# Dilated values: stored order in group 0, 512 columns wide in groups 1 and 2, made between the last latent blocks; four gates between dilated blocks

## The chip, the cores and the metric

One core of one Trainium2 chip runs the whole program. The metric is the device time of one execution in microseconds (us); several executions are summed up by their median. TensorE (PE) multiplies, ScalarE (ACT) and VectorE (DVE) do the arithmetic around it, GpSimd (POOL) casts and fills a few tiles, and SyncE (SP) issues nearly all loads from memory.

## The reference, cut to what matters

Four layers work on 512 tokens of 1024 features. Only the first two, of one kind (`first_block`), are touched by the change. In each of them a normalised input `h` is multiplied by `w_in`, and three kinds of attention read the product; each result is projected, multiplied by a gate and added up:

```python
y_a = mla_mixer(c_q, c_kv, k_r, ...)              # latent attention, 8 heads
y_b = dilated_mixer(q_b, k_b, qkv_b[:, :, 2])     # 12 heads: 3 groups of 4, dilation 1, 4, 16
y_c = neighbourhood_mixer(qkv_c[:, :, 0], ...)    # 8 heads
gates = sigmoid(gate_logits).reshape(B, S, 3, D_MODEL)
merged = gates[:, :, 0] * (y_a @ w_pa[l]) + gates[:, :, 1] * (y_b @ w_pb[l]) + gates[:, :, 2] * (y_c @ w_pc[l])
x = x + merged @ w_o[l]
```

The values of the dilated attention are `h @ w_in` at 3 x 256 columns (group 0, 1, 2). A query of group 0 sees keys within 64 tokens; in group 1 tokens whose numbers agree modulo 4 see each other, in group 2 modulo 16. A softmax over the three groups' log sums weights their outputs, which is the same as one softmax over all the keys of the three groups together, and so the kernel does it.

## The kernel before, in words

The tokens are stored in an order `NA_TOK` that suits the neighbourhood attention. `h` lies in SBUF transposed: eight tiles of 128 features x 512 tokens, each split into a high and a low part (`r` tiles, fp32r), and each product is three matmuls (`mm3`: high by high, high by low, low by high). Weights are streamed: SP loads 128 x 1024 numbers into one of three `raw` tiles, ACT casts the high part into one of two `whi` tiles, DVE subtracts the low part into `wlo`, and 24 matmuls read them (a unit).

A layer runs three pipelines of attention blocks one after the other: `mla` (latent, 32 blocks), `dil` (dilated, 4 head positions `j` x 4 query blocks `b` = 16 blocks) and `na` (neighbourhood, 32 blocks). Each block has a `before` list (work that is written ahead of it), a `score` part and a `rest` part, which follows one or two blocks later. The order on each engine is not the order in which the code is written: a scheduler sorts the instructions when the program is built, and can pull matmuls that wait for nothing in among earlier attention blocks.

`vproj` makes values: `h` is the stationary operand (128 features x 128 tokens are loaded into PE), 256 columns of weights stream past it. For the three dilated groups (`order4`) a token block is every fourth stored token (`m4(a)[:, b]`), so the 128 numbers of a partition that PE loads lie four elements (16 bytes) apart. For the neighbourhood's two groups the 128 tokens lie side by side. A group is 8 feature tiles x 4 token blocks x 3 matmuls = 96 matmuls. All three dilated groups are written ahead of the first dilated block. `roped` makes the rotated queries and keys, and writes them in the same order by four.

A gate is one unit (`gate`): 24 matmuls of 512 columns, a DVE multiplication by the norm, an ACT tanh. The gates of the dilated branch are made in `merge(1, ...)`, which runs as a filler inside the neighbourhood blocks.

PSUM has eight banks, in two lists: `AB` (five) for attention blocks, `MB` (three) for everything else. Lists of tiles (`Slots`) are handed out first in, first out when the program is built.

At the program's start three loads of the masks pass through the same three `raw` tiles as the weights, and POOL casts them to bf16; the third unit of weights can be loaded when the first mask has been cast.

Of the kernel before, what the change touches and what calls it, by code (L numbers as in the profile page):

```python
# [38 lines left out]
def _shape_constants():  # L39
    f = np.float32  # L40

    def inv_freq(dim):
        e = (-np.arange(0, dim, 2, dtype=f) / f(dim)).astype(np.float64)
        return np.power(10000.0, e).astype(f)

    def angles(tok, inv):
        return (tok.astype(f)[None, :] * inv[:, None]).astype(f)

    a = angles(NA_TOK, inv_freq(32))
    c, s = np.cos(a), np.sin(a)  # L50
    mla = np.stack([np.tile(np.concatenate([c, c]), (4, 1)), np.tile(np.concatenate([-s, s]), (4, 1))], 1)


    tok4 = NA_TOK.reshape(128, 4).T.reshape(-1)
    a = angles(tok4, inv_freq(64))
    c, s = np.cos(a), np.sin(a)
    dil = np.stack([np.tile(np.concatenate([c, c]), (2, 1)), np.tile(np.concatenate([-s, s]), (2, 1))], 1)

    half = (f(1) / np.power(10000.0, (np.arange(128, dtype=f) / f(128)).astype(np.float64)).astype(f)).astype(f)
    a = angles(_IDX, half)  # L60
    ret = np.stack([np.cos(a), np.sin(a)], 1)

    t0 = NA_TOK.reshape(128, 4)[:, 0]
    diff = t0[:, None] - t0[None, :]
    ms = [np.where(np.abs(diff - d) <= 64, f(0), f(NEG)) for d in range(-3, 4)]
    l = t0 // 4
    ms.append(np.where(np.abs(l[:, None] - l[None, :]) <= 64, f(0), f(NEG)))
    ms.append(np.where((l[:, None] - l[None, :]) % 4 == 0, f(0), f(NEG)))
    masks = np.concatenate(ms, 1).astype(f)

    k = np.arange(128, dtype=np.float64)
    q = np.arange(S, dtype=np.float64)
    rel = q[None, :] - k[:, None]
    lg = np.log1p(-np.exp2(-5.0 - np.arange(4)))
    decay = np.stack([np.where(rel >= 0, np.exp(np.maximum(rel, 0) * g), 0.0) for g in lg], 1).astype(f)

    return {
        "t_mla": mla.astype(f), "t_dil": dil.astype(f), "t_ret": ret.astype(f),
        "t_mask": masks, "t_dec": decay, "t_id": np.eye(128, dtype=f),
    }  # L80
# [58 lines left out]
def layout(inp):  # L139
# [24 lines left out]
    o["w_in0"] = np.stack([_wide(w[:, cols[:512]]) for w in a["w_in"]])  # L164
    o["w_v"] = np.stack([w[:, vcols].reshape(DK, 128, 5, 256).transpose(2, 1, 0, 3) for w in a["w_in"]])
    uq = []
# [60 lines left out]
def kernel(ctx: ExitStack, tc: tile.TileContext, d, out):  # L227
# [9 lines left out]
    FX = [pool.tile([128, S], F32, name=f"x{i}") for i in range(8)]  # L237
    FA = Slots([pool.tile([128, S], F32, name=f"fa{i}") for i in range(10)])
    FM = Slots([pool.tile([128, S], F32, name=f"fm{i}") for i in range(5)])
# [8 lines left out]
    cols = pool.tile([128, NCOL], F32, name="cols")  # L248
    masks = pool.tile([128, 9 * 128], BF16, name="masks")
    epsc = pool.tile([128, 1], F32, name="epsc")  # L250
    smalls = Slots([pool.tile([128, 8], F32, name=f"sm{i}") for i in range(10)])
    rcols = Slots([pool.tile([128, 16], F32, name=f"rc{i}") for i in range(6)])

# [369 lines left out]
    def first_layer(l, xsrc, h, norm, ahead=()):  # L623
# [24 lines left out]
        def gate(i, m, z):  # L648
            gate_scaled(i, m, z)
            gate_tanh(z)  # L650

        def merge(i, y, wname, m0, early):

            nkt = len(y)
            w = None
            for m in (m0, m0 + 1):
                z = merged[m]
                if not early:
                    z = FM.get()
                    gate(i, m, z)  # L660
# [8 lines left out]
                if not early:  # L669
                    gt(merged[m], merged[m], z, ALU.add)  # L670
                    FM.put(z)
            if m0 == 6:
# [271 lines left out]

        def vproj(g, order4):

            v = [R.get(), R.get()]
            pss = [MB.get(), MB.get()]
            for u in range(2):
                w = wload(d["w_v"][l, g, :, 4 * u:4 * u + 4, :].rearrange("p k c -> p (k c)"), 1024)  # L950
                for b in range(4):
                    for i in range(4):
                        k = 4 * u + i
                        lt = tuple(m4(a)[:, b] if order4 else a[:, b * 128:b * 128 + 128] for a in hp[k])
                        wv = tuple(a[:, i * 256:i * 256 + 256] for a in w)
                        mm3(pss[b // 2][:, (b % 2) * 256:(b % 2) * 256 + 256], lt, wv, k == 0 and b % 2 == 0, k == 7 and b % 2 == 1)
            for b in range(4):
                c = (8 if order4 else 0) + b
                value_split(pss[b // 2][:, (b % 2) * 256:(b % 2) * 256 + 256], v, b, 1, norm.rc[:, c:c + 1])
            MB.put(*pss)  # L960
            return v

        def roped(i):
            ps = chunk(i)
            z, zs = FA.get(), FA.get()
            nc.scalar.copy(out=b4(z), in_=m4(ps))
            MB.put(ps)
            for g in range(4):
                nc.sync.dma_start(out=zs[32 * g:32 * g + 32], in_=z[32 * (g ^ 1):32 * (g ^ 1) + 32])
            tt(z, z, st["cs"][0])  # L970
            tt(zs, zs, st["cs"][1])
            tt(z, z, zs, ALU.add)
# [3 lines left out]
        def dil_qk0(p):  # L976
            for w in range(2):
                z = roped(6 * p + w)
                st[("q0", "k0")[w], p] = stack_k(z) if w else stack_q(z, 0.125)
                FA.put(z)  # L980
# [18 lines left out]

        def dil_v(g):  # L1000
            st["vg", g] = vproj(g, True)

        yb = [None] * 2

        def dil_block(j, b):
# [3 lines left out]
            if (j, b) == (0, 0):  # L1009
                before += [dil_tables, lambda: dil_qk0(0), lambda: dil_q12(0), lambda: dil_k12(0)]  # L1010
                before += [lambda: dil_v(0), lambda: dil_v(1), lambda: dil_v(2)]
            if j == 0:
                before += [fill]
            if (j, b) == (1, 0):
                before += [lambda: dil_q12(1), lambda: dil_k12(1)]
# [8 lines left out]
            def score():  # L1024
# [7 lines left out]
                bk["p"] = pt = PT.get()  # L1032
                nc.vector.tensor_tensor_reduce(out=pt[:, :512], in0=s0, in1=masks[:, (3 - b) * 128:(7 - b) * 128], scale=1.0,
                                               scalar=-3e38, op0=ALU.add, op1=ALU.max, accum_out=sm[:, 0:1])
                nc.vector.tensor_tensor_reduce(out=pt[:, 512:768], in0=s1[:, :256], in1=masks[:, 896:1152], scale=1.0,
                                               scalar=-3e38, op0=ALU.add, op1=ALU.max, accum_out=sm[:, 1:2])
# [71 lines left out]
        def na_v(g):  # L1108
            st["vc", g] = vproj(3 + g, False)

# [91 lines left out]
        na = [na_block(p, e, qb) for p in range(4) for e in range(2) for qb in range(4)]  # L1202

        pipeline(mla, PD[0])
        add_merge(0, ya, "w_pa", True)
        pipeline(dil, PD[1])
# [61 lines left out]
    for i in range(3):  # L1268
        raw = RAW.get()
        nc.scalar.dma_start(out=raw[:, :384], in_=d["t_mask"][:, 384 * i:384 * i + 384])  # L1270
        nc.gpsimd.tensor_copy(out=masks[:, 384 * i:384 * i + 384], in_=raw[:, :384])
        RAW.put(raw)
# [283 lines left out]
```

## Time and profile before

| what | value |
|---|---|
| time, median of 3 runs (lowest to highest) | 3324.41 us (3324.07 to 3324.78) |
| the profiled execution's own time | 3323.28 us |
| its span on the core | 3321.5 us, mean granted clock 0.999 |
| PE busy | 3290.6 us (99%), 15970 matmuls |
| DVE busy / ACT busy | 1812.7 us (55%) / 1454.0 us (44%) |
| DMA | 313.77 MB, 94 GB/s on average |

Some 1.8 us of the profiled execution's time lie outside its span. A matmul's row shows when it was issued and for how long it was under way; since matmuls overlap, what one costs is the distance from its start to the next one's.

### The profile page before, as it was taken

The page shows a single profiled execution, that of the slowest core. Times are in us where ns is not written, and L with a number is a line of the kernel's source. Part 1 is how long each engine was busy: PE and PEld are TensorE (multiplying, and loading weights), DVE is VectorE, ACT ScalarE, POOL GpSimd, SP SyncE. Part 2 cuts the span into 40 slices and gives each one's busy share as a digit, 9 for nine tenths or more (in the row PEclk, how much of TensorE's full clock was granted, in tenths as well). Part 3 has the DMA queues.
Part 4 walks back from the last instruction along what each step waited for, and adds up shares of the span by engine and source line. Part 5 has one row for each costly group of instructions (what it writes and reads, how often), then busy time and mean ns, then how long its engine had stood idle before and what let it go on. Part 6 is the DMA issues. An engine that isn't in the chain of part 4 may idle for free.

```text
span 3321.5 us, 40467 instructions
## 1 busy us (share of the span) xinstructions
PE 3290.6 (99%) x15970; PEld 2791.7 (84%) x15970; DVE 1812.7 (55%) x3018; ACT 1454.0 (44%) x2345; POOL 124.3 (4%) x127
## 2 busy tenths in 40 slices
PE   9999999999999999999999999999999999999999
PEld 7898888888888898888888888888888888788887
DVE  6847874555347748765454265554433257743323
ACT  5735763332236626653333234443423247742222
POOL 0000001011000000010111000000000000000000
PEclk9999999999999999999999999999999999999999
DMA  4113223323333123323223322223133332222332
GB/s 161 52 51 101 92 88 109 109 96 96 110 110 92 54 62 100 103 80 122 94 95 111 121 76 80 80 86 121 58 101 105 111 109 83 95 77 95 99 105 89
DMA packets 97439, 313.77 MB, mean 94 GB/s; under 512 B 12000, under 2 KB 16736, under 8 KB 97248
## 3 DMA queue, kind: packets, MB, share of 16 engines
q1 hardware_dynamic: 95376, 308.33, 29.2%
q8 instruction: 125, 2.05, 0.2%
q10 hardware_dynamic: 1872, 2.85, 0.2%
q14 instruction: 66, 0.54, 0.1%
HBM read 298.55 MB, written 4.19 MB: 91 GB/s over the span
## 4 chain that ended last, share of the span: by engine, by line
PE 90%; DVE 4%; ACT 4%; DMA 1%; issue 1%; DVEq 0%; SPq 0%; ACTq 0%
PE b L283 28%; PE b L285 28%; PE b L284 28%; PE b L715 1%; PE b L714 1%; ACT r L270 1%; DVE wlo L271 1%; DVE r L271 1%; DVE fa L277 1%; ACT whi L270 1%; PE b L1170 1%; DMA raw<-in_l_in_dram 1%; PE b L903 1%; DMA raw<-in_gu_dram 0%; ACT fa L508 0%
## 5 line engine op out<-in xcount | busy, mean ns | idle before, releaser
L283 PE MATMUL b<-r,whi 128*128 128x512 f32 (+1 forms) x3032 | 1164.2, 388 | 8.9 <-ACT whi L270 3.3
L284 PE MATMUL b<-r,whi 128*128 128x512 f32 (+1 forms) x3032 | 1169.3, 387 | 0.0
L285 PE MATMUL b<-r,wlo 128*128 128x512 f32 (+1 forms) x3032 | 1161.8, 387 | 0.0
L270 ACT CAST whi<-raw 128x1024 fp32r<-128x1024 f32 (+2 forms) x486 | 506.7, 1043 | 1200.3 <-PE b L284 680.5
L271 DVE TENSOR_TENSOR wlo<-raw,whi 128x1024 fp32r<-128x1024 f32 (+2 forms) x486 | 633.8, 1304 | 625.6 <-ACT whi L270 618.9
L283 PEld LDWEIGHTS b<-r,whi 128*128 128x128 f32 x3032 | 567.1, 188 | 122.1 <-ACT whi L270 4.6
L285 PEld LDWEIGHTS b<-r,wlo 128*128 128x128 f32 x3032 | 570.6, 188 | 111.4
L284 PEld LDWEIGHTS b<-r,whi 128*128 128x128 f32 x3032 | 570.4, 188 | 109.4
L284 PE MATMUL b<-wlo,r 128*128 128x512 f32 (+1 forms) x1040 | 393.2, 378 | 0.5 <-DVE wlo L271 0.5
L285 PE MATMUL b<-whi,r 128*128 128x512 f32 (+1 forms) x1040 | 393.4, 378 | 0.0
L283 PE MATMUL b<-whi,r 128*128 128x512 f32 (+1 forms) x1040 | 322.4, 378 | 1.4 <-ACT whi L270 1.4
L283 PEld LDWEIGHTS b<-whi,r 128*128 128x128 f32 x1040 | 222.5, 214 | 30.4 <-ACT whi L270 2.3
L284 PEld LDWEIGHTS b<-wlo,r 128*128 128x128 f32 x1040 | 222.7, 214 | 29.3 <-DVE wlo L271 0.9
L285 PEld LDWEIGHTS b<-whi,r 128*128 128x128 f32 x1040 | 222.9, 214 | 28.0
L283 PE MATMUL b<-r,r 128*128 128x512 f32 (+4 forms) x640 | 226.3, 357 | 6.2 <-ACT p L694 5.4
L284 PE MATMUL b<-r,r 128*128 128x512 f32 (+4 forms) x640 | 224.8, 352 | 0.1
L285 PE MATMUL b<-r,r 128*128 128x512 f32 (+4 forms) x640 | 223.6, 351 | 0.0
L277 DVE TENSOR_TENSOR fm<-b,fa 128x512 f32<-128x512 f32 x120 | 82.7, 691 | 235.1 <-PE b L285 235.0
L277 DVE TENSOR_TENSOR fa<-fa,fa 128x512 f32<-128x512 f32 x202 | 135.6, 695 | 62.7 <-ACT fa L1392 29.0
L271 DVE TENSOR_TENSOR r<-b,r 128x512 fp32r<-128x512 f32 (+3 forms) x264 | 146.9, 570 | 40.0 <-ACT r L270 38.8
L270 ACT CAST r<-b 128x512 fp32r<-128x512 f32 (+3 forms) x264 | 125.2, 495 | 94.2 <-PE b L903 29.3
L277 DVE TENSOR_TENSOR fm<-b,fm 128x512 f32<-128x512 f32 (+2 forms) x86 | 59.1, 687 | 175.2 <-PE b L285 136.0
(168 smaller groups left out, 2938.6 us busy)
## 6 DMA issues: line engine op xcount, KB each, us to landing
raw<-in_gu_dram SPq DMA_DIRECT2D x176, 512.0 KB, 3.4
raw<-in_w_in_dram SPq DMA_DIRECT2D x96, 512.0 KB, 3.5
raw<-in_f_out_dram SPq DMA_DIRECT2D x44, 512.0 KB, 3.4
raw<-in_r_in_dram SPq DMA_DIRECT2D x32, 512.0 KB, 3.4
raw<-in_l_in_dram SPq DMA_DIRECT2D x24, 512.0 KB, 3.4
raw<-in_w_tok_dram SPq DMA_DIRECT2D x22, 512.0 KB, 3.5
raw<-in_w_v_dram SPq DMA_DIRECT2D x20, 512.0 KB, 3.8
raw<-in_r_v_dram SPq DMA_DIRECT2D x16, 512.0 KB, 3.9
```

Source lines behind the costliest of these rows:

```text
L270: nc.scalar.copy(out=hi, in_=src)
L271: nc.vector.tensor_tensor(out=lo, in0=src, in1=f(hi), op=ALU.subtract)
L277: nc.vector.tensor_tensor(out=out_, in0=a, in1=b, op=op)
L283: nc.tensor.matmul(ps, lhsT=l[0], rhs=r[0], start=start, stop=False)
L284: nc.tensor.matmul(ps, lhsT=l[0], rhs=r[1], start=False, stop=False)
L285: nc.tensor.matmul(ps, lhsT=l[1], rhs=r[0], start=False, stop=stop)
L714: nc.tensor.matmul(o, lhsT=lt, rhs=ph, start=start, stop=False)
L715: nc.tensor.matmul(o, lhsT=lt, rhs=pl, start=False, stop=stop)
L903: nc.tensor.transpose(tp[:, k * 128:k * 128 + 128], b["p"][:, k * 128:k * 128 + 128], ident)
L1170: nc.tensor.transpose(t0[:, k * 128:k * 128 + 128], pt[:, k * 128:k * 128 + 128], ident)
```

## The change

Group 0's values, its keys (`k0`) and its masks now take the stored order of the tokens; its queries keep the order by four. Groups 1 and 2 share one product with 512 weight columns (`vproj_by4`, weights `w_vw`), in four parts of one unit each, which are written into the `before` lists of latent blocks 25, 27, 29 and 31. They accumulate in four banks at once, so one bank moves from `AB` to `MB` during the latent pipeline and back after it. Group 0 stays ahead of the first dilated block. The gates 0 to 3 of the dilated branch are made ahead of the blocks of `j == 3` and kept in four `FA` tiles until `merge` uses them. Masks grow from 9 to 18 blocks of 128 columns; to make room `FA`, `smalls` and `rcols` shrink.

```diff
-    ms = [np.where(np.abs(diff - d) <= 64, f(0), f(NEG)) for d in range(-3, 4)]
+    ms = [np.where(np.abs(t0[:, None] + b - NA_TOK[None, :]) <= 64, f(0), f(NEG)) for b in range(4)]
...
-    FA = Slots([pool.tile([128, S], F32, name=f"fa{i}") for i in range(10)])
+    FA = Slots([pool.tile([128, S], F32, name=f"fa{i}") for i in range(9)])
...
+        made = {}
+
+        def gate_early(m):
+
+            made[m] = FA.get()
+            gate(1, m, made[m])
...
-                z = merged[m]
-                if not early:
+                z, home = merged[m], FM
+                if i == 1 and m in made:
+                    z, home = made[m], FA
+                elif not early:
...
-        def vproj(g, order4):
+        def vproj(g):
...
-                        lt = tuple(m4(a)[:, b] if order4 else a[:, b * 128:b * 128 + 128] for a in hp[k])
+                        lt = tuple(a[:, b * 128:b * 128 + 128] for a in hp[k])
...
+        def vproj_by4(done):
+
+            pss = []
+
+            def part(u):
+                if u == 0:
+                    pss.extend(MB.get() for _ in range(4))
+                w = wload(d["w_vw"][l, :, 2 * u:2 * u + 2, :].rearrange("p k c -> p (k c)"), 1024)
+                for b in range(4):
+                    for i in range(2):
+                        k = 2 * u + i
+                        lt = tuple(m4(a)[:, b] for a in hp[k])
+                        mm3(pss[b], lt, tuple(a[:, i * 512:i * 512 + 512] for a in w), k == 0, k == 7)
+                if u < 3:
+                    return
+                vs = [[R.get(), R.get()] for _ in range(2)]
+                for b in range(4):
+                    for i in range(2):
+                        value_split(pss[b][:, i * 256:i * 256 + 256], vs[i], b, 1, norm.rc[:, 8 + b:9 + b])
+                    MB.put(pss[b])
+                done(*vs)
+
+            return [lambda u=u: part(u) for u in range(4)]
...
-            tt(z, z, st["cs"][0])
-            tt(zs, zs, st["cs"][1])
+            for t, c in zip((z, zs), st["cs"]):
+                tt(t if order4 else m4(t), t if order4 else m4(t), c if order4 else b4(c))
...
-                before += [lambda: dil_v(0), lambda: dil_v(1), lambda: dil_v(2)]
+                before += [dil_v0]
...
+            if j == 3:
+                before += [lambda: gate_early(b)]
...
+        MB.put(AB.get())
+        for i, part in enumerate(vproj_by4(dil_v12)):
+            mla[25 + 2 * i][0].append(part)
         pipeline(mla, PD[0])
+        AB.put(MB.get())
...
-        nc.scalar.dma_start(out=raw[:, :384], in_=d["t_mask"][:, 384 * i:384 * i + 384])
-        nc.gpsimd.tensor_copy(out=masks[:, 384 * i:384 * i + 384], in_=raw[:, :384])
+        nc.scalar.dma_start(out=raw[:, :768], in_=d["t_mask"][:, 768 * i:768 * i + 768])
+        nc.gpsimd.tensor_copy(out=masks[:, 768 * i:768 * i + 768], in_=raw[:, :768])
```

What the scheduler makes of it is seen in the order of PE's instructions. The first place is the end of the dilated values in layer 0. Before the change they end in a long run of matmuls of 256 columns (`whi`, `wlo` streaming past `h`, the `r` tiles) directly ahead of the projection `w_pa` of the latent output (the last three rows, of 512 columns):

```order
L283 MATMUL b_133<-whi_94,r_68 128x256
L284 MATMUL b_133<-wlo_96,r_68 128x256
L285 MATMUL b_133<-whi_94,r_68 128x256
L283 MATMUL b_133<-whi_94,r_69 128x256
L284 MATMUL b_133<-wlo_96,r_69 128x256
L285 MATMUL b_133<-whi_94,r_69 128x256
L283 MATMUL b_133<-whi_94,r_70 128x256
L284 MATMUL b_133<-wlo_96,r_70 128x256
L285 MATMUL b_133<-whi_94,r_70 128x256
L283 MATMUL b_126<-r_72,whi_93 128x512
L284 MATMUL b_126<-r_72,whi_93 128x512
L285 MATMUL b_126<-r_72,wlo_95 128x512
```

Now groups 1 and 2 stand among the latent blocks, with 512 columns. In this piece of the second half of the latent pipeline, L913 is a block's transposes of its probabilities (L903 before), and the twelve rows between are one token block's share of the first two parts, of which the last two are left out here:

```order
L913 MATMUL b_126<-ident,p_122 128x128 x4
L284 MATMUL b_125<-whi_93,r_63 128x512
L285 MATMUL b_125<-wlo_95,r_63 128x512
L286 MATMUL b_125<-whi_93,r_63 128x512
L284 MATMUL b_125<-whi_93,r_64 128x512
L285 MATMUL b_125<-wlo_95,r_64 128x512
L286 MATMUL b_125<-whi_93,r_64 128x512
L284 MATMUL b_125<-whi_94,r_65 128x512
L285 MATMUL b_125<-wlo_96,r_65 128x512
L286 MATMUL b_125<-whi_94,r_65 128x512
L284 MATMUL b_125<-whi_94,r_66 128x512
```

In a layer, 96 matmuls of 512 columns take the place of 192 of 256. Group 0's 96 of 256 columns stay where the first piece stands.

The second place is the program's start on PE: the end of the second unit of weights (`r_66`) and the beginning of the third (`r_67`). Before, the matmuls that sum the squares of the input norm (L378, by `ones`) come in behind eight matmuls of the third unit, one of them here and seven later:

```order
L285 MATMUL b_130<-r_66,wlo_96 128x512
L283 MATMUL b_127<-r_67,whi_93 128x512
L284 MATMUL b_127<-r_67,whi_93 128x512
L283 MATMUL b_128<-r_67,whi_93 128x512
L284 MATMUL b_128<-r_67,whi_93 128x512
L283 MATMUL b_129<-r_67,whi_93 128x512
L284 MATMUL b_129<-r_67,whi_93 128x512
L283 MATMUL b_130<-r_67,whi_93 128x512
L284 MATMUL b_130<-r_67,whi_93 128x512
L378 MATMUL b_132<-ones,r_71 128x2
```

Now all eight (L379) stand ahead of the third unit's first matmul:

```order
L284 MATMUL b_129<-r_66,whi_94 128x512
L285 MATMUL b_129<-r_66,whi_94 128x512
L286 MATMUL b_129<-r_66,wlo_96 128x512
L379 MATMUL b_131<-ones,r_71 128x2 x8
L284 MATMUL b_126<-r_67,whi_93 128x512
L285 MATMUL b_126<-r_67,whi_93 128x512
```

They read `r_71`, the split sum of squares, which ACT and DVE have to finish first.

## Rows read from the trace of the kernel before

**Rows 1.** The page's first part: busy time, share and instructions of each engine

```profile
span 3321.5 us, 40467 instructions
...
PE 3290.6 (99%) x15970; PEld 2791.7 (84%) x15970; DVE 1812.7 (55%) x3018; ACT 1454.0 (44%) x2345; POOL 124.3 (4%) x127
```

**Rows 2.** Waits of PE over the whole span: total us, times, longest

```profile
PE b L283 <- ACT p L694: 5.4, 7, 1.7
...
PE b L750 <- DVE sm L1153: 2.4, 2, 1.2
```

**Rows 3.** Order of time, PE, dilated values, four in a row: start us, us, engine, line

```profile
208.97 0.40 PE L285 MATMUL b<-whi,r 128*128 128x256 f32 x1
...
209.68 0.40 PE L285 MATMUL b<-whi,r 128*128 128x256 f32 x1
```

**Rows 4.** Order of time, PE, neighbourhood values, four in a row

```profile
433.56 0.28 PE L284 MATMUL b<-wlo,r 128*128 128x256 f32 x1
...
433.92 0.28 PE L284 MATMUL b<-wlo,r 128*128 128x256 f32 x1
```

**Rows 5.** Weight loads (PEld) by shape, dilated values, then neighbourhood values

```profile
L283 PEld LDWEIGHTS b<-whi,r 128*128 128x128 f32 x55 | 18.1, 330 | 0.0
...
L283 PEld LDWEIGHTS b<-whi,r 128*128 128x128 f32 x17 | 3.3, 192 | 0.0
```

**Rows 6.** Order of time, PE: a score's last (512), then two dilated value matmuls

```profile
179.71 0.40 PE L285 MATMUL b<-r,r 96*128 96x512 f32 x1
179.94 0.28 PE L285 MATMUL b<-whi,r 128*128 128x256 f32 x1
180.06 0.39 PE L283 MATMUL b<-whi,r 128*128 128x256 f32 x1
```

**Rows 7.** By stretch: us, busy of PE, PEld, DVE, ACT, POOL, clock, DMA

```profile
10.00:12.00 2.00, 2.00 (x6) 1.51 (x6) 1.90 (x4) 2.00 (x4) 0.00 (x0) 0.50 1.06 375
...
205.00:243.50 38.50, 38.50 (x166) 38.50 (x166) 7.75 (x11) 6.50 (x10) 0.00 (x0) 1.00 0.12 41
1172.00:1203.00 31.00, 31.00 (x134) 31.00 (x134) 7.64 (x11) 5.81 (x10) 0.00 (x0) 1.00 0.16 51
...
100.00:120.00 20.00, 18.86 (x113) 15.68 (x112) 19.44 (x39) 16.82 (x37) 0.00 (x0) 1.00 0.15 41
...
88.00:205.00 117.00, 113.96 (x620) 101.68 (x620) 90.06 (x167) 80.71 (x160) 4.16 (x8) 1.00 0.19 55
365.00:500.00 135.00, 133.81 (x766) 116.45 (x765) 101.80 (x267) 92.11 (x198) 9.60 (x11) 1.00 0.29 92
```

**Rows 8.** DVE and ACT by shape, 85 to 205 us

```profile
L891 DVE TENSOR_REDUCE sm<-b 128x1 f32<-128x512 f32 x28 | 19.1, 682 | 1.2 <-PE b L285 0.9
...
L694 ACT ACTIVATE p<-b,sm 128x512 f32<-128x512 f32 x29 | 20.1, 691 | 1.7 <-DVE sm L695 1.0 <-DVE sm L891 0.6
L270 ACT CAST r<-b 128x512 fp32r<-128x512 f32 x34 | 19.7, 584 | 16.7 <-PE b L903 13.6 <-PE b L714 2.8
```

**Rows 9.** Order of time, the program's start: POOL, ACT, DVE, PE

```profile
13.37 0.84 POOL L1271 CAST masks<-raw 128x384 bf16<-128x384 f32 x1 [12.93 <-DMA raw<-in_t_mask_dram]
...
17.82 1.05 ACT L270 CAST whi<-raw 128x1024 fp32r<-128x1024 f32 x1 [0.93 <-issue]
...
20.89 0.68 DVE L271 TENSOR_TENSOR r<-fa,r 128x512 fp32r<-128x512 f32 x1
...
20.15 0.39 PE L283 MATMUL b<-r,whi 128*128 128x512 f32 x1
```

**Rows 10.** Order of time, DVE: the dilated tables, scaled by a reordered norm

```profile
62.04 2.05 DVE L277 TENSOR_TENSOR fa<-fa,fa 128x512 f32<-128x512 f32 x2
64.01 0.68 DVE L277 TENSOR_TENSOR x<-b,fa 128x512 f32<-128x512 f32 x1
```

**Rows 11.** Order of time, PE: a gate's matmuls, first and last of 18

```profile
455.89 0.39 PE L284 MATMUL b<-r,whi 128*128 128x512 f32 x1
...
459.75 0.39 PE L283 MATMUL b<-r,whi 128*128 128x512 f32 x1
```

More of the change, by code (lines that the diff above doesn't have):

```diff
@@ L63, in _shape_constants @@
     t0 = NA_TOK.reshape(128, 4)[:, 0]
-    diff = t0[:, None] - t0[None, :]
-    ms = [np.where(np.abs(diff - d) <= 64, f(0), f(NEG)) for d in range(-3, 4)]
+    ms = [np.where(np.abs(t0[:, None] + b - NA_TOK[None, :]) <= 64, f(0), f(NEG)) for b in range(4)]
     l = t0 // 4
@@ L164, in layout @@
     o["w_in0"] = np.stack([_wide(w[:, cols[:512]]) for w in a["w_in"]])
-    o["w_v"] = np.stack([w[:, vcols].reshape(DK, 128, 5, 256).transpose(2, 1, 0, 3) for w in a["w_in"]])
+    vone = np.concatenate([vcols[:256], vcols[768:]])
+    o["w_v"] = np.stack([w[:, vone].reshape(DK, 128, 3, 256).transpose(2, 1, 0, 3) for w in a["w_in"]])
+    o["w_vw"] = np.stack([w[:, vcols[256:768]].reshape(DK, 128, 512).transpose(1, 0, 2) for w in a["w_in"]])
     uq = []
@@ L248 @@
     cols = pool.tile([128, NCOL], F32, name="cols")
-    masks = pool.tile([128, 9 * 128], BF16, name="masks")
+    masks = pool.tile([128, 18 * 128], BF16, name="masks")
     epsc = pool.tile([128, 1], F32, name="epsc")
-    smalls = Slots([pool.tile([128, 8], F32, name=f"sm{i}") for i in range(10)])
-    rcols = Slots([pool.tile([128, 16], F32, name=f"rc{i}") for i in range(6)])
+    smalls = Slots([pool.tile([128, 8], F32, name=f"sm{i}") for i in range(9)])
+    rcols = Slots([pool.tile([128, 16], F32, name=f"rc{i}") for i in range(4)])
     def small():
@@ L670, in merge @@
                     gt(merged[m], merged[m], z, ALU.add)
-                    FM.put(z)
+                    home.put(z)
             if m0 == 6:
@@ L957, in vproj, with roped @@
             for b in range(4):
-                c = (8 if order4 else 0) + b
-                value_split(pss[b // 2][:, (b % 2) * 256:(b % 2) * 256 + 256], v, b, 1, norm.rc[:, c:c + 1])
+                value_split(pss[b // 2][:, (b % 2) * 256:(b % 2) * 256 + 256], v, b, 1, norm.rc[:, b:b + 1])
             MB.put(*pss)
             return v
-        def roped(i):
+        def vproj_by4(done):
[18 more added lines that the diff above has]
+            return [lambda u=u: part(u) for u in range(4)]
+        def roped(i, order4=True):
             ps = chunk(i)
             z, zs = FA.get(), FA.get()
-            nc.scalar.copy(out=b4(z), in_=m4(ps))
+            nc.scalar.copy(out=b4(z) if order4 else z, in_=m4(ps) if order4 else ps)
             MB.put(ps)
@@ L977, in dil_qk0 @@
             for w in range(2):
-                z = roped(6 * p + w)
+                z = roped(6 * p + w, w == 0)
                 st[("q0", "k0")[w], p] = stack_k(z) if w else stack_q(z, 0.125)
@@ L998, in dil_k12, with dil_v0, dil_v12 @@
             FA.put(z)
-        def dil_v(g):
-            st["vg", g] = vproj(g, True)
+        def dil_v0():
+            st["vg", 0] = vproj(0)
+        def dil_v12(v1, v2):
+            st["vg", 1], st["vg", 2] = v1, v2
         yb = [None] * 2
@@ L1032, in score @@
                 bk["p"] = pt = PT.get()
-                nc.vector.tensor_tensor_reduce(out=pt[:, :512], in0=s0, in1=masks[:, (3 - b) * 128:(7 - b) * 128], scale=1.0,
+                nc.vector.tensor_tensor_reduce(out=pt[:, :512], in0=s0, in1=masks[:, b * 512:b * 512 + 512], scale=1.0,
                                                scalar=-3e38, op0=ALU.add, op1=ALU.max, accum_out=sm[:, 0:1])
-                nc.vector.tensor_tensor_reduce(out=pt[:, 512:768], in0=s1[:, :256], in1=masks[:, 896:1152], scale=1.0,
+                nc.vector.tensor_tensor_reduce(out=pt[:, 512:768], in0=s1[:, :256], in1=masks[:, 2048:2304], scale=1.0,
                                                scalar=-3e38, op0=ALU.add, op1=ALU.max, accum_out=sm[:, 1:2])
@@ L1108, in na_v @@
         def na_v(g):
-            st["vc", g] = vproj(3 + g, False)
+            st["vc", g] = vproj(1 + g)
         def na_qk(p, w):
```

## The prediction

> **What bounds the kernel now.** I read the page's first part, then PE's waits, then PE's order of time where the values are made, then the stretches of the attention stages. PE is busy 99% of the span, while DVE stands at 55% and ACT at 44% [rows 1]. PE's waits are few and short: the largest kind, for a softmax ahead of a latent score, is 5.4 us in seven waits [rows 2], and all its idle time is 3321.5 - 3290.6 = 30.9 us [rows 1]. So the time is the sum of what PE's matmuls cost in a row, and a change counts if it alters that sum, or if it makes PE wait where it doesn't wait now.
>
> A busy PE is not yet a PE at its peak, and here the rows show it. In the dilated values four matmuls of 256 columns start within 0.71 us, 0.237 us apart [rows 3]; over the clean stretch of 38.5 us there are 165 of them after the one under way at its start, 0.233 us each [rows 7]. In the neighbourhood's values four matmuls of the same shape start within 0.36 us, 0.120 us apart [rows 4]. The difference between the two is the order of the stationary tokens: every fourth token, or 128 side by side. It is seen on the weight loads: 330 ns beside 192 ns, without idle time in either stretch [rows 5]. And the first kind costs as much as a matmul of 512 columns, 3.86 us over 17 steps = 0.227 us [rows 11]. So a dilated value matmul is as long as its weight load, and its 256 columns hide beneath it.
>
> **The change part by part.**
>
> *Removed:* 3 groups x 96 = 288 matmuls a layer at 0.233 us: 67.1 us.
>
> *Group 0 in stored order:* 96 matmuls with tokens side by side. That is exactly the shape of the neighbourhood's values: 96 x 0.120 = 11.5 us.
>
> *Groups 1 and 2 in one:* 96 matmuls of 512 columns with the spaced load. No row of before has this pair. From below the price is that of any 512-column matmul, 0.227 us; from above, the load and the columns follow each other: 0.233 + (0.227 - 0.120) = 0.340 us, the wider matmul's extra columns in full. The rows decide between them: a score of 512 columns is followed by a value matmul with a spaced load, and that one starts 0.23 us after the score's last matmul and is under way 0.28 us, as short as [rows 4], and the next starts 0.12 us later [rows 6]. So its spaced load had run beneath 512 streaming columns and nothing of it was left. I take 0.235 us, the load's own rhythm or the score's [rows 6], whichever is longer: 96 x 0.235 = 22.6 us.
>
> A rule of the Trainium skill speaks against this: in "TensorE: Matmul & The Clock Gate", part 3 on packing, it says that a weight load overlaps matmuls in flight only when its row group differs. All loads here take all 128 rows, so by it the upper price of 0.340 would hold. The trace does not agree: 3 x 0.12 us for matmuls whose loads are 192 ns each leaves no room for a load outside the matmuls.
>
> The saving on PE is 67.1 - 11.5 - 22.6 = 33.0 us a layer, 66.0 us for both.
>
> *Placement among the latent blocks.* Matmuls that wait for nothing cost the same wherever they stand. Before, the scheduler had already pulled some 120 of the 288 dilated value matmuls and the first four query and key units into the latent stage, 28 us and 4 x 24 x 0.227 = 21.8 us. By the new order it takes the 96 wide ones, some 40 of group 0's and the same four units, 22.6 + 4.8 + 21.8 us: about the same cover, with about the same work for DVE (90.1 of 117 us in that stage, ACT 80.7) [rows 7]. What ends the blocks' chain is the softmax: reduce 0.68, exp 0.69, and the transposed probabilities' split, 0.58 on ACT and on DVE about as long as the reduce [rows 8].
>
> *One bank fewer for latent attention (five to four).* A block holds a score bank over three matmuls, the reduce and the exp, 0.7 [rows 6] + 0.68 + 0.69 = some 2.1 us, and a transpose bank over four transposes (0.12 us each by the narrow matmuls [rows 4], an estimate) and the split, 0.5 + 0.58 + 0.68 = 1.8 us [rows 8]; an output bank, held for some two of four blocks, adds about 2 us a block. That is 6 us of bank a block, and the stage has 117 us for 32 blocks, 3.7 us each: 1.6 banks at work, and twice that if every step waits as long as it works. Four are enough on average; in a burst one is short now and then. I put 1 us a layer on it, 2 in all, with bounds from -5.4 (the waits for softmax go away in both layers) [rows 2] to the rival's price below.
>
> *The program's start.* The masks' loads and casts double. The first cast ends at 14.2 us and sets free the tile of the third weight unit; two masks' additional 0.39 MB at 375 GB/s are 1.0 us [rows 7], and a second cast's worth is 0.84 us, so it ends some 1.9 us later. The unit's high part, ready at 18.87 us, would be ready near 20.8, and PE reaches the unit at 20.15 us [rows 9]. Besides, all the norm's small matmuls now stand ahead of the unit. They read the split whose DVE half started at 20.89 and took 0.68 us, behind another subtraction that now comes after it, so it would be ready near 21.2. Both end the same wait: 1.2 us, once. From below it is nothing, from above 3 us if the loads are late as well.
>
> *Costed at nothing:* The four early gates are the same matmuls in other blocks. The neighbourhood stage that loses them has 4 x 24 x 0.227 = 21.8 us less filler, and DVE's 101.8 us of its 135 [rows 7] still fit; PE's one wait for a score there is 1.2 us a layer [rows 2], and as much again is the price if cover is lost. Four DVE multiplications a layer for the keys go through reordered operands: two such take 2.05 us together where contiguous ones take 0.68 each [rows 10], so some 0.35 us more each, 1.4 us a layer on an engine that is busy 55% of the span [rows 1]. Fewer `FA` tiles tie bias loads to the query and key tiles before them on SP's queue; weights queued behind have three tiles' lead of 5.4 us each.
>
> **The sum.** The profiled execution took 3323.28 us. 3323.28 - 66.0 + 2.0 + 1.2 = 3260.5 us. The median of the runs shown is 1.1 us above the profiled execution: 3261.6, predicted as 3261 us. About 0.2% (6.6 us) is what a measurement of this kernel can tell from no change; the forecast is ten times that.
>
> **The rivals.**
>
> *Load and columns in sequence.* The wide matmul costs 0.340 us. Against it stands the pair in [rows 6]; for it, that no row has the pair in a steady run. 96 x 2 x 0.105 = 20.2 us more: 3281 us. Chance 0.07.
>
> *Stored order is not what makes the load short.* If the 330 ns came from something else in that stage, group 0 would keep 0.233: 2 x 96 x 0.113 = 21.7 us more, 3283 us. Against it: layer 1's stretch has the same rhythm, 31 us over 133 matmuls, with other traffic beside it [rows 7], and the short ones [rows 4] differ in nothing but the tokens' spacing. The Trainium skill's formula for the load in "TensorE: Matmul & The Clock Gate" (columns over 1.2, whatever their spacing) points this way; its figure, an estimate of 107 ns for 128 columns, would leave the dilated matmuls unexplained. Chance 0.03.
>
> *Four banks set the pace of the latent stage.* Banks are handed out in a fixed turn, so one late split holds up the next score even while another bank is free; DVE is already at 19.4 of 20 us in the densest stretch [rows 7]. If the stage grew by a tenth, that is 11.7 us a layer: 3323.28 - 66.0 + 1.2 + 23.4 + 1.1 = 3283 us; chance 0.11 for anything from 8 us in all to break-even. It decides from 66.0 - 1.2 = 65 us on, 1.0 us for each of 64 blocks: at 1.1 us a block 70.4 us are lost, and the time is 3330 us, slower than before. Chance 0.02.
>
> **Chances and range.** The forecast's own range is 3253 (wide matmuls at 0.227, 1.5 us; no start wait, 1.2; softmax waits gone in both layers, 5.4) to 3270 (start 3, a few more waits), chance 0.76; 0.01 is left for what I don't see. Half of the bank rival lies below 3278, so 3253 to 3278 holds a little over 8 in 10. Faster 0.97, same 0.01, slower 0.02, from the same cases.
>
> **What would show it.** PE should have 192 matmuls fewer, 15778. In the latent stage weight loads of some 310 to 330 ns should stand beside 512-column matmuls that start 0.23 to 0.24 us apart; ahead of the first dilated block 96 matmuls 0.12 us apart with loads of 190 ns. PE's idle time should stay near 31 us, with a wait of about 1 us near 20 us. If the wide matmuls stand 0.34 us apart, the first rival holds; if waits of scores or transposes on ACT and DVE grow by tens of us between 80 and 180 us, the banks do. The prediction is wrong if the time is above 3270 with wide matmuls at 0.235, for then the waits that I put at 3 us are what I misjudged.

## The result, and the profile after

The changed kernel takes 3274.69 us (median of four runs, 3270.97 to 3277.68), beside 3324.6 us for the kernel before on the same chip: the ratio is 0.9848, its 95% interval 0.9835 to 0.9860. The time lies within the predicted range, 13.7 us above the predicted point. The profiled execution took 3276.36 us.

The page's first part after, to be read beside [rows 1]:

```profile
span 3274.6 us, 40093 instructions
...
PE 3232.8 (99%) x15778; PEld 2726.3 (83%) x15778; DVE 1820.0 (56%) x3018; ACT 1454.3 (44%) x2345; POOL 126.8 (4%) x127
```

The 192 matmuls are gone and PE's busy time is 57.8 us shorter, but its idle time has grown from 30.9 to 3274.6 - 3232.8 = 41.8 us. PE's waits over the whole span (total us, times, longest), beside [rows 2]:

```profile
PE b L284 <- ACT r L271: 4.8, 2, 3.4
...
PE b L913 <- DVE fm L278: 3.4, 4, 1.5
PE b L913 <- ACT p L704: 3.3, 6, 0.9
PE b L379 <- ACT r L271: 2.9, 1, 2.9
PE b L284 <- DVE r L272: 2.8, 8, 0.6
```

L913 is a block's transposes and L379 the norm's sum at the program's start; neither was among the large waits of before. `fm` at L278 is the sum that empties an output bank, and `r` at L272 the split that empties a transpose or product bank: what ends the waits of the last line, and of L913 for `fm`, is not the operand but a bank that is read to its end. The two waits of the first line, 1.4 and 3.4 us, stand at 1882 and 2779 us, in a part of the program that the change does not touch (part C below).

The predicted prices of the matmuls, in order of time on PE. The wide ones in the latent stage (start us, us, engine, line):

```profile
172.21 0.40 PE L284 MATMUL b<-whi,r 128*128 128x512 f32 x1
172.44 0.40 PE L285 MATMUL b<-wlo,r 128*128 128x512 f32 x1
172.69 0.39 PE L286 MATMUL b<-whi,r 128*128 128x512 f32 x1
172.92 0.40 PE L284 MATMUL b<-whi,r 128*128 128x512 f32 x1
173.15 0.40 PE L285 MATMUL b<-wlo,r 128*128 128x512 f32 x1
...
210.83 0.28 PE L284 MATMUL b<-whi,r 128*128 128x256 f32 x1
210.95 0.28 PE L285 MATMUL b<-wlo,r 128*128 128x256 f32 x1
211.07 0.28 PE L286 MATMUL b<-whi,r 128*128 128x256 f32 x1
```

Four steps of the wide ones take 0.94 us, 0.235 each; the last three rows are group 0 ahead of the first dilated block, 0.12 us apart. The weight loads by shape, first in the wide stretch, then in group 0's (busy us, mean ns):

```profile
L286 PEld LDWEIGHTS b<-whi,r 128*128 128x128 f32 x7 | 2.2, 309 | 0.0
...
L286 PEld LDWEIGHTS b<-whi,r 128*128 128x128 f32 x23 | 4.4, 192 | 0.0
```

So all three prices of matmuls hold. **Where the rest went** is seen by cutting the span at three starts on PE: the first matmul of layer 0's `w_o`, of layer 1's `w_in` and of its `w_o`. Part A runs from the start to layer 0's `w_o`, part B from layer 1's `w_in` to its `w_o`; these two hold all that the change touches. Between them lie 403.9 to 404.0 us in every kernel. Part C is the rest, with the same instructions in all of them. S is the start of the third weight unit; the last column counts stretches of part C with the granted clock at 1.2 GHz, half of full speed (the program's end, where PE has no work, left out). All are of profiled executions:

| kernel | S | A | B | C | span | clock falls in C |
|---|---|---|---|---|---|---|
| before | 20.1 | 565.6 | 555.3 | 1796.6 | 3321.5 | 0 |
| changed | 23.5 | 540.3 | 527.3 | 1803.0 | 3274.6 | 2 |
| `e1_masks_own_tiles` | 20.2 | 540.7 | 528.9 | 1799.2 | 3272.7 | 1 |
| `e2_wide_after_latent` | 23.1 | 538.1 | 522.1 | 1801.0 | 3265.2 | 1 |
| `e3_before_four_banks` | 20.5 | 578.8 | 571.1 | 1797.9 | 3351.8 | 1 |
| `e4_gates_late` | 23.2 | 542.2 | 530.9 | 1796.9 | 3274.0 | 0 |
| `e6_both_bank_and_masks` | 20.1 | 533.5 | 523.7 | 1801.8 | 3262.9 | 2 |
| `e7_group0_by_four` | 23.1 | 551.0 | 538.1 | 1800.2 | 3293.2 | 1 |
| `e8_changed_again` | 23.1 | 538.6 | 527.4 | 1802.7 | 3272.7 | 3 |
| `e9_bank_from_block_24` | 23.2 | 533.8 | 522.4 | 1796.3 | 3256.5 | 0 |
| `e10_block_24_and_masks` | 18.7 | 531.2 | 522.4 | 1800.4 | 3257.9 | 1 |
| `e11_bank_from_block_12` | 23.4 | 536.6 | 525.3 | 1800.8 | 3266.7 | 2 |

The prediction's terms give 33.0 - 1.2 - 1 = 30.8 us saved in A and 32.0 in B. Measured are 25.3, 28.0, and 6.4 lost in C. Each row is one execution; the changed kernel, taken twice, differs by 1.7 us in A, 0.1 in B and 0.3 in C.

### The profile page after: what moved, and what is told of

The parts are those of the page before. It is cut to its first block, busy times and chain, and to the rows that moved or that the text cites. A ratio compares the mean times of both kernels' runs of the same rounds, so it can differ in the third digit from the quotient of the medians.

```text
span 3274.6 us, 40093 instructions
## 1 busy us (share of the span) xinstructions
PE 3232.8 (99%) x15778; PEld 2726.3 (83%) x15778; DVE 1820.0 (56%) x3018; ACT 1454.3 (44%) x2345; POOL 126.8 (4%) x127
## 4 chain that ended last, share of the span: by engine, by line
PE 89%; DVE 4%; ACT 4%; DMA 1%; issue 1%; DVEq 0%; SPq 0%; ACTq 0%
PE b L284 28%; PE b L285 28%; PE b L286 28%; PE b L725 1%; PE b L724 1%; DVE r L272 1%; DVE fa L278 1%; ACT r L271 1%; DVE wlo L272 1%; PE b L1209 1%; DMA raw<-in_gu_dram 1%; PE b L913 1%; ACT whi L271 1%; DMA raw<-in_l_in_dram 0%; ACT fa L509 0%
## 5 line engine op out<-in xcount | busy, mean ns | idle before, releaser
L284 PE MATMUL b<-r,whi 128*128 128x512 f32 (+1 forms) x3032 | 1164.8, 388 | 10.7 <-ACT r L271 4.8
L272 DVE TENSOR_TENSOR wlo<-raw,whi 128x1024 fp32r<-128x1024 f32 (+2 forms) x486 | 632.9, 1302 | 606.3 <-ACT whi L271 600.9
L285 PE MATMUL b<-wlo,r 128*128 128x512 f32 (+1 forms) x976 | 360.5, 369 | 0.5 <-DVE wlo L272 0.5
L286 PE MATMUL b<-whi,r 128*128 128x512 f32 (+1 forms) x976 | 360.3, 369 | 0.0
L284 PE MATMUL b<-whi,r 128*128 128x512 f32 (+1 forms) x976 | 293.7, 373 | 4.7 <-DVE r L272 1.7
L286 PE MATMUL b<-r,r 128*128 128x512 f32 (+4 forms) x640 | 223.2, 351 | 0.0
L284 PEld LDWEIGHTS b<-whi,r 128*128 128x128 f32 x976 | 191.0, 196 | 36.0 <-DVE r L272 3.1
L285 PEld LDWEIGHTS b<-wlo,r 128*128 128x128 f32 x976 | 191.9, 197 | 29.3 <-DVE wlo L272 0.9
L286 PEld LDWEIGHTS b<-whi,r 128*128 128x128 f32 x976 | 191.8, 196 | 28.0
L278 DVE TENSOR_TENSOR fm<-b,fa 128x512 f32<-128x512 f32 x112 | 77.2, 691 | 232.0 <-PE b L286 232.0
L278 DVE TENSOR_TENSOR fa<-fa,fa 128x512 f32<-128x512 f32 (+1 forms) x202 | 139.6, 716 | 47.7 <-ACT fa L1435 20.2
L272 DVE TENSOR_TENSOR r<-b,r 128x512 fp32r<-128x512 f32 (+3 forms) x264 | 146.1, 570 | 34.7 <-ACT r L271 33.3
L278 DVE TENSOR_TENSOR fm<-b,fm 128x512 f32<-128x512 f32 (+2 forms) x86 | 59.1, 687 | 167.4 <-PE b L286 135.3
```

What stands on the lines that cost most here:

```text
L272: nc.vector.tensor_tensor(out=lo, in0=src, in1=f(hi), op=ALU.subtract)
L278: nc.vector.tensor_tensor(out=out_, in0=a, in1=b, op=op)
L284: nc.tensor.matmul(ps, lhsT=l[0], rhs=r[0], start=start, stop=False)
L285: nc.tensor.matmul(ps, lhsT=l[0], rhs=r[1], start=False, stop=False)
L286: nc.tensor.matmul(ps, lhsT=l[1], rhs=r[0], start=False, stop=stop)
```

## The experiments

The theory after the result: the bank that the latent stage gives up costs several us a layer, not one. Rivals: the start, the early gates, or a price of a matmul that is wrong elsewhere.

**The masks through tiles of their own** (`e1_masks_own_tiles`): the three loads pass through `PT` tiles, and the third weight unit no longer waits for POOL.

```diff
-        raw = RAW.get()
+        raw = PT.get()
...
-        RAW.put(raw)
+        PT.put(raw)
```

> The changed kernel, but the three mask loads pass through the probability tiles, which are free at the start, and not through the weight tiles. Theory: the doubled loads and casts hold back the third weight unit and its norm matmuls; the first PE wait near 20 us and the half-clock stretch after it go, 4 us in all, and the time is about 3271 us (the changed kernel has 3274.7). Rival: the wait near 20 us is that of the norm matmuls' place in the order, whatever the masks do: about 3274 us, and the gap between second and third unit is still some 3 us.

Measured: 3275.71 us, ratio to before 0.9850 (0.9835 to 0.9864), no gain. The start did what was meant: S went from 23.5 to 20.2 us. These are stretches of the changed kernel, then of this one (busy us of PE, PEld, DVE, ACT, POOL, then granted clock and DMA):

```profile
20.00:24.00 4.00, 1.84 (x9) 1.72 (x10) 2.92 (x5) 1.90 (x4) 0.00 (x0) 0.87 0.04 15
24.00:28.00 4.00, 4.00 (x14) 3.15 (x13) 1.92 (x6) 0.86 (x1) 0.00 (x0) 0.70 0.79 258
```

```profile
20.00:24.00 4.00, 4.00 (x19) 3.32 (x18) 3.76 (x4) 1.68 (x2) 0.34 (x1) 1.00 0.34 117
24.00:28.00 4.00, 4.00 (x20) 3.32 (x19) 1.22 (x1) 1.05 (x1) 0.00 (x0) 1.00 0.46 150
```

But part A is 540.7 beside 540.3 us. Where both have done the same number of matmuls of each kind, this kernel is 3.9 us ahead at 48.4 us and 2.9 at 88.2; the first dilated score starts at 223.2 us beside 222.9. What was won ahead of the latent stage was lost within it. So each side held in part: the wait went, as in the theory, and the time stayed, as in the rival.

**The wide matmuls behind the latent stage** (`e2_wide_after_latent`). The latent blocks keep five banks; the fourth bank of the products is borrowed only for the wide part, which stands ahead of the first dilated block.

```diff
+                before += [lambda: MB.put(AB.get())] + vproj_by4(dil_v12) + [lambda: AB.put(MB.get())]
...
-        MB.put(AB.get())
-        for i, part in enumerate(vproj_by4(dil_v12)):
-            mla[25 + 2 * i][0].append(part)
...
-        AB.put(MB.get())
```

> The changed kernel, but the wide values stand ahead of the first dilated block, behind the latent pipeline, and take the fourth bank only there, so that latent attention has five banks again. Theory (four banks cost the latent stage): the waits of transposes and scores for banks go, 6 to 12 us less over both layers: 3263 to 3269 us. Rival (the latent stage loses because of what fills it, not because of banks): without the wide parts as filler PE waits more for softmax, and the time is 3275 us or more.

Measured: 3265.57 us, 0.9821 (0.9806 to 0.9836), 9 us under the changed kernel and inside the theory's range. Part B falls by 5.2 us, part A by 2.2, with a clock fall in its latent stage (from 142.7 us on).

**The kernel before with a bank fewer** (`e3_before_four_banks`): only the move of the bank is added to it.

```diff
+        MB.put(AB.get())
         pipeline(mla, PD[0])
+        AB.put(MB.get())
```

> The kernel before with one edit: latent attention has four banks and the rest four, as in the changed kernel. Theory (four banks cost the latent stage): 6 to 12 us more than before, 3331 to 3337 us, with waits of scores and transposes for a bank's last reader. Rival: within 2 us of before, 3323 to 3327 us.

Measured: 3352.9 us, 1.0081 (1.0066 to 1.0096), 27 us slower than before. That is more than the theory or its rival said: part A +13.2, B +15.8. The stretches show that waits are not all of it:

```profile
96.00:104.00 8.00, 5.58 (x31) 4.00 (x30) 7.37 (x15) 7.36 (x17) 0.00 (x0) 1.00 0.19 66
104.00:108.00 4.00, 3.75 (x15) 3.27 (x16) 2.28 (x6) 2.24 (x4) 0.00 (x0) 0.60 0.02 4
124.00:128.00 4.00, 3.02 (x17) 2.19 (x17) 3.28 (x8) 3.21 (x9) 0.00 (x0) 1.00 0.00 0
128.00:136.00 8.00, 6.57 (x21) 5.51 (x22) 4.48 (x10) 4.39 (x9) 0.00 (x0) 0.57 0.01 2
```

Behind the two stretches in which PE waited the mean granted clock is 0.60 and 0.57; in part of each it is 1.2 GHz, and matmuls of 512 columns start 0.43 us apart there instead of 0.23. PE's idle time grew by 15.1 us and its busy time by as much. Two more such falls stand behind the latent stages, at 1357 us in part B and at 2859 us in C; that the missing bank brings those is not shown.

**No early gates** (`e4_gates_late`): the gates go back into `merge`.

```diff
-            if j == 3:
-                before += [lambda: gate_early(b)]
```

> The changed kernel without the early gates; they are made in the merges among the neighbourhood blocks, as before. Theory: nothing that counts, 3272 to 3277 us, since PE's work is the same and neither stage waited. Rival: the dilated stage, or the neighbourhood stage that lost this cover, waits because of them: 4 us or more less than the changed kernel if the first, more if the second.

Measured: 3277.28 us, 0.9858 (0.9842 to 0.9875), 2.6 us above the changed kernel, just above the theory's range and short of the rival's 4 us. In the profile a wait of PE is back, that of a neighbourhood score for the instruction that reads an earlier score's bank (layer 0, at 352 us):

```profile
PE b L760 <- DVE sm L1190: 1.2, 1, 1.2
```

The same wait stands in layer 1 at 1287 us, and [rows 2] have both. Part A rises by 1.9 us, B by 3.6 (1.7 of it a clock fall in its latent stage): some 2 us a layer, of which the wait is 1.2.

**Both repairs together** (`e6_both_bank_and_masks`: the edits of `e1_masks_own_tiles` and `e2_wide_after_latent`).

> The changed kernel with the two repairs of the first batch together: the mask tables pass through tiles of their own, and the wide value matmuls stand behind the latent stage, which keeps its five banks. Theory A, the bank loss and the start loss are separate: the third weight unit starts near 20.2 us instead of 23.5 and the projection's start stays 4 to 5 us earlier, so 3265.6 - 4 = 3261.5 us (3259 to 3264). Theory B, what is won at the start is given back in the latent stage, as in the run with the masks alone (first dilated score 223.2 against 222.9 us there): 3265.6 us (3264 to 3268), and the latent stage loses some 4 us more than in the run with the wide part moved.

Measured: 3264.03 us, 0.9818 (0.9804 to 0.9831), on the border of the two theories. Part A is 4.6 us shorter than with the wide part moved alone (1.7 of it by a clock fall at 23 us that is missing here), B 1.6 and C 0.8 us longer. The gain was kept where it arose, but only 1.5 us of it show in the median.

**Group 0 back in order by four** (`e7_group0_by_four`), its masks and keys too:

```diff
-                        lt = tuple(a[:, b * 128:b * 128 + 128] for a in hp[k])
+                        lt = tuple(m4(a)[:, b] if g == 0 else a[:, b * 128:b * 128 + 128] for a in hp[k])
```

> The changed kernel with group 0's values, masks and keys again in order by four, groups 1 and 2 as changed. Theory A, the step of four columns is what makes the loads of the value projection long: the 96 matmuls of group 0 in a layer go from 0.120 us apart back to 0.233, 10.8 us a layer and 21.7 us in all, so 3274.7 + 21.7 = 3296 us (3292 to 3300), with loads of 310 to 330 ns in front of the first dilated block. Rival B, the order in which the columns are read is not what counts: 3271 to 3279 us, with starts 0.23 us apart in the changed kernel's group 0 explained by something else.

Measured: 3296.55 us, 0.9917 (0.9903 to 0.9930), where theory A said 3296. Beside the changed kernel part A grows by 10.7 us and B by 10.8, where 10.8 a layer were worked out. Group 0's matmuls on PE, then their weight loads by shape:

```profile
222.15 0.40 PE L286 MATMUL b<-whi,r 128*128 128x256 f32 x1
222.38 0.40 PE L284 MATMUL b<-whi,r 128*128 128x256 f32 x1
222.62 0.40 PE L285 MATMUL b<-wlo,r 128*128 128x256 f32 x1
```

```profile
L286 PEld LDWEIGHTS b<-whi,r 128*128 128x128 f32 x22 | 7.3, 330 | 0.0
```

The same instructions at the same place are 0.235 us apart with every fourth token as the stationary operand and 0.12 with tokens side by side.

**The bank given up later** (`e9_bank_from_block_24`). The wide part stays among the last latent blocks, but the bank passes in front of block 24, not in front of the stage.

```diff
-        MB.put(AB.get())
+        mla[24][0].append(lambda: MB.put(AB.get()))
```

> The changed kernel, but the fifth bank of the transposes passes to the matmuls in front of latent block 24 and not in front of the whole stage; the wide part stays among the last blocks. Theory A, a bank fewer costs its 7.4 us a layer spread over all 32 blocks: a quarter of it is left, some 1.8 us a layer, so 3274.7 - 11 = 3264 us (3261 to 3267). Rival B, the cost lies where the four parts of the wide projection stand, which hold all four banks of the matmuls there: 3273 to 3278 us, with the latent stage's loss still near 13 us.

Measured: 3258.06 us, 0.9802 (0.9789 to 0.9815), the fastest of all and 17 us under the changed kernel measured beside it (`e8_changed_again`; its expectation was

> The changed kernel itself, unaltered, beside the other three on the same chip, to be compared with them: 3271 to 3278 us by every theory.

and it took 3274.81 us, 0.9847). That is below theory A's range and far below rival B's. Of the 16.2 us between the two profiled spans, 4.8 lie in part A, 5.0 in B and 6.4 in C, so what the bank's two stages gave back is 9.8, near the 11 of theory A. PE's idle time falls by 3.7 us in part A and 3.5 in B; the scheduler also sorts PE's instructions in another order with the bank kept longer, and whether the remaining 2.6 us come of that is not shown. The page's first part, then stretches that cover the latent stage:

```profile
span 3256.5 us, 40113 instructions
...
PE 3226.8 (99%) x15778; PEld 2725.5 (84%) x15778; DVE 1817.9 (56%) x3018; ACT 1452.1 (45%) x2345; POOL 127.3 (4%) x127
```

```profile
88.00:130.00 42.00, 40.73 (x231) 34.38 (x230) 37.94 (x74) 35.04 (x72) 0.00 (x0) 1.00 0.15 45
130.00:160.00 30.00, 28.50 (x154) 26.00 (x153) 21.36 (x40) 20.36 (x42) 0.00 (x0) 1.00 0.16 44
160.00:216.00 56.00, 56.00 (x326) 50.68 (x326) 41.15 (x66) 34.90 (x62) 4.17 (x8) 1.00 0.28 85
```

The changed kernel's latent stage in the same view:

```profile
88.00:130.00 42.00, 39.50 (x216) 32.05 (x215) 36.64 (x70) 32.52 (x67) 0.00 (x0) 1.00 0.15 44
130.00:170.00 40.00, 35.71 (x186) 31.41 (x186) 25.76 (x49) 24.21 (x48) 0.00 (x0) 1.00 0.12 34
170.00:222.00 52.00, 52.00 (x309) 46.99 (x308) 40.28 (x66) 35.03 (x62) 4.16 (x8) 1.00 0.30 92
```

PE is idle for 6.8 us in the changed kernel's stage, 2.8 us here, as before (3.0) [rows 7]. The idle time lies ahead of 170 us, before most of the wide part; from there on PE is full in both. One of the changed kernel's waits, in order of time, with ACT, DVE and PE:

```profile
141.05 0.71 ACT L707 ACTIVATE p<-p,sm 128x512 f32<-128x512 f32 x1
...
141.79 0.58 ACT L730 COPY fm<-b 64x512 f32<-64x512 f32 x1
141.91 0.47 DVE L709 TENSOR_SCALAR p<-p,sm 128x512 f32<-128x512 f32 x1
142.42 0.69 DVE L278 TENSOR_TENSOR fm<-b,fm 64x512 f32<-64x512 f32 x1
...
143.16 0.66 PE L913 MATMUL b<-ident,p 128*128 128x128 f32 x4 [1.45 <-DVE fm L278]
```

The last probabilities were ready at 142.38 us (141.91 + 0.47), and PE stood idle since 141.71. The transposes start 0.05 us after the sum has read an output bank to its end (142.42 + 0.69 = 143.11), and the sum had to follow ACT's copy, which stood behind a softmax on ACT.

**From block 12 on** (`e11_bank_from_block_12`: 12 in place of 24) and **block 24 with the masks apart** (`e10_block_24_and_masks`).

> As the kernel with the bank passed from block 24 on, but from block 12 on. Theory A, a bank fewer costs the same for every block that it lacks: 13.2 us of loss in the stage with it gone from the start, 7.25 us with it gone from block 24 on, so about 10.2 us with it gone from block 12 on, 3 us a layer more than 7.25 and 3258.1 + 6 = 3264 us (3262 to 3267). Rival B, only the first blocks pay, in which the masked heads stand and DVE is busy for 12.3 of 15 us: 3257 to 3260 us. Rival C, only the blocks behind the twelfth pay: 3268 to 3275 us.

> The kernel with the bank passed from block 24 on, with the mask tables through tiles of their own as well. Theory A, the start's gain survives where the latent stage has its five banks: 4 us were won in front of the latent stage and 1.5 us were left of them in the two kernels with the wide part moved (3265.6 and 3264.0 us), so 3258.1 - 1.5 = 3256.5 us (3254 to 3258). Rival B, DVE and ACT, which are the busiest in the first half of the latent stage, set its pace, and what comes earlier into it waits in it: 3257 to 3260 us.

Measured: 3270.55 us, 0.9837 (0.9824 to 0.9851), and 3259.38 us, 0.9803 (0.9790 to 0.9816). From block 12 on, parts A and B are 2.8 and 2.9 us longer than from block 24 on. That is what theory A gave for them (3 a layer), although the time is 6.6 us above its 3264 and in the range of rival C: part C, which the rival does not speak of, is 4.5 us longer, with two clock falls. With the masks apart A is 2.6 us shorter, B the same, C 4.1 us longer with one fall. The times cannot be told apart; they are in rival B's range, but the gain in A is not given back as rival B has it.

## Why the prediction was right, and what was mis-sized

The time lies in the range of 3253 to 3278 us, but above the forecast's own range, which ends at 3270: it lies in the part that was added for the rival of the banks. Two of the shifts were in no term, 4 us gained by the gates and 6.4 lost in part C, so that the number is met owes something to luck. The forecast of what bounds the kernel and of what the matmuls cost held.

**Prices of the matmuls: right.** 0.235 for the wide ones and 0.120 for group 0, from [rows 6] and [rows 4], were met in the trace, and `e7_group0_by_four` undoes one of them for 21.7 us (beside `e8_changed_again`) of the 21.7 worked out. So the first rival falls by the order of time, and the second by that run: the spacing of the stationary tokens is what makes the load long. The rule of the Trainium skill that was weighed there ("TensorE: Matmul & The Clock Gate", part 3) is not borne out by the wide matmuls: loads of 309 ns over all 128 rows, beneath matmuls 235 ns apart, leave no room for a load outside them.

**"I put 1 us a layer on it, 2 in all": the term that was mis-sized.** The sign named for it came: a time above 3270 with wide matmuls at 0.235, by which the prediction calls itself wrong on its waits. The third rival came true at its small end. Of parts A and B, 33.0 us and the gates' 2 a layer should be left; with 2.4 taken by the start in A (below), 7.3 us are missing in A and 7.0 in B, 14.3 in all as a remainder. `e8_changed_again` gives 7.3 and 7.1. Reckoned in the same way, 4.8 and 5.0 us a layer are missing with the bank gone from block 12 on, 1.5 and 2.1 with it gone from block 24 on: some 0.2 us on average for each block that lacks it. So the price is spread over the stage, and it is nowhere near the 1.0 us a block at which the banks would decide the sign; that stands as forecast.

The average of banks at work, 1.6 of five, doubled, was the wrong measure: banks are taken in a fixed turn, and in the wait shown above the transposes stood for a bank that ACT and DVE were late to empty. [Rows 7] had a stretch with DVE at 19.4 of 20 us, and I gave it to the rival instead of the sum. [Rows 2] held a second sign, which I read as a wait for a softmax that might go away. A score reads queries and keys alone, so what it waits for in an earlier block's exp (L694) is the bank that the exp reads. The longest of these waits before, in order of time (ACT, then PE):

```profile
137.91 0.69 ACT L694 ACTIVATE p<-b,sm 128x512 f32<-128x512 f32 x1
...
138.75 0.50 PE L283 MATMUL b<-r,r 96*128 96x512 f32 x1 [1.68 <-ACT p L694]
```

So the stage was short of banks now and then with five already: three such waits make 2.7 of the 3.0 us for which PE is idle in layer 0's stage before.

**"1.2 us, once" for the start: the wait was longer, its price 2.4 and 0.7 us in two executions.** The wait was looked for in the right place. The order of time of the changed kernel (DVE, then ACT, then PE):

```profile
19.60 1.40 DVE L278 TENSOR_TENSOR fa<-fa,fa 128x512 f32<-128x512 f32 x2
21.04 0.62 ACT L271 CAST r<-fa 128x512 fp32r<-128x512 f32 x1 [3.99 <-DVE fa L278]
21.56 1.04 ACT L271 CAST whi<-raw 128x1024 fp32r<-128x1024 f32 x1
...
21.71 0.27 PE L379 MATMUL b<-ones,r 128*128 128x2 f32 x1 [2.87 <-ACT r L271]
...
23.49 0.77 PE L284 MATMUL b<-r,whi 128*128 128x512 f32 x1
```

PE is idle for 2.87 us, then for 0.45 more, and the eight small matmuls stand ahead of the unit; behind it the clock is 0.70. The weights' cast, which ends at 22.60, was late as well. Where both kernels have done the same number of matmuls of each kind, the changed one is 3.9 us behind at 52.6 us. At 89.1, ahead of the latent stage, it is 2.4 us behind, since a wait of before is gone that stood between:

```profile
70.13 0.51 PE L283 MATMUL b<-r,whi 128*128 128x512 f32 x1 [1.17 <-DVE r L271]
```

Of the 2.4 us, 1.7 are the clock's (0.13 x 4 + 0.30 x 4, from the stretches shown with the first experiment), which I had not counted. In `e8_changed_again` the clock's fall stands at 8.2 to 11.6 us, as it does before the change (8.6 to 12.0), PE is idle for 1.18 and 0.45 us at the same place, and 0.7 us are left ahead of the latent stage. The repair of the masks changed the time measurably in none of three pairs.

**Gates "costed at nothing": a gain.** I took the wait of a neighbourhood score, 1.2 us a layer, as a measure of the price if cover is lost; in the changed kernel it is this wait that is gone, and the gates' place is worth 2 us a layer. Why it goes is not shown.

**Part C** was forecast unchanged and holds 6.4 us of loss. The table shows what it goes with: 1796.3 to 1796.9 us without a clock fall, in three kernels; 1797.9 to 1801.0 with one; 1800.8 to 1803.0 with two or three. PE's idle time in it is 15.5 us before and 19.0 in the changed kernel. The 14 falls of the table stand at only four places of part C: 411 to 412 us behind its start (five of them), 1188 to 1190 (four), 1305 to 1310 (four) and 1432 (one). At the first, PE waits 1.4 us in the changed kernel and 0.5 us in `e9_bank_from_block_24`, which has no fall there. It is not chance alone: the mean granted clock of the whole span is 0.997 or 0.998 in all nine executions of the changed kernel, 0.999 in all four of `e9_bank_from_block_24`, and 0.999 or more in 20 of 25 of before. Why the same instructions wait longer in one kernel than in another is open.

The sum of the profiled executions is 66.0 + 4 - 2.4 - 14.3 - 6.4 = 46.9 us, in which the banks' term is what the others leave. `e9_bank_from_block_24` saves 65.0 us in its span, close to the prediction's sum without the bank's price (66.0 - 1.2), but by other terms: what the gates win about pays for what is left of the bank's and the start's.

## What to carry to other kernels

What is shorter on a full engine arrives in full only if its neighbours keep their buffers. Before a bank is lent, see whether scores or transposes wait for banks already; the average number of banks at work does not tell. Lend it as late as it is needed, since here the price grew with the number of blocks that lacked it. A stationary operand with its numbers four apart sets the pace of matmuls of 256 columns (0.235 us against 0.120); beneath 512 columns it costs next to nothing (0.235 against 0.227). Where several us are to be told apart, compare parts of the span between fixed landmarks, and times at which the same matmuls are done: here the part that no kernel changes took 1796.3 to 1803.0 us.

## What the runs showed of the hardware that was not expected

- A wait of PE can cost more than its length. In `e3_before_four_banks`, behind stretches in which PE was idle for 2.4 and 1.0 us (5.58 busy of 8, 3.02 of 4), the granted clock lay near 0.6 of full speed (1.2 GHz in part of the stretch), and the same matmuls took longer. One bank less in the kernel before was 15.1 us of idle time and 15.2 us of longer busy time with the same matmuls; summed over stretches of 4 us, (1 - clock) x 4 us is 15.6 there and 2.0 before (the program's last 4 us left out), which accounts for 13.6 of the 15.2. The length of one wait does not decide it: in the changed kernel one of 1.44 us at 1882 us has such a stretch behind it, one of 3.39 us at 2779 us has none.
- A spaced load hides beneath long matmuls, but not wholly behind a block's 128-column transposes. In the changed kernel's order of time the wide matmul that follows them is under way for 0.60 us and the next one starts 0.44 us later, in all six places where it does not wait. A matmul of 512 columns without the spacing is under way for 0.47 to 0.48 us there and the next one starts 0.31 to 0.32 us later, in all twenty. The first kind, then the second:

```profile
146.23 0.60 PE L913 MATMUL b<-ident,p 128*128 128x128 f32 x4
146.59 0.60 PE L284 MATMUL b<-whi,r 128*128 128x512 f32 x1
147.03 0.40 PE L285 MATMUL b<-wlo,r 128*128 128x512 f32 x1
...
89.87 0.47 PE L284 MATMUL b<-r,whi 128*128 128x512 f32 x1
90.19 0.39 PE L285 MATMUL b<-r,whi 128*128 128x512 f32 x1
```
